# Up projection of a seven-product MLP with joined 512-column matmuls, sums kept in PSUM, and weight sums built in one buffer

## The chip, the core and the metric

The kernel runs on one core of a Trainium2 chip. The metric is the device time of one execution in microseconds (us). Before the change three runs gave 2035.43, 2039.5 and 2040.1 us, a median of 2039.5 us. Five engines work side by side, each on its own list of instructions in order: PE (TensorE, matmuls; its weight loads are listed as PEld), DVE (VectorE), ACT (ScalarE), POOL (GpSimd) and SP (SyncE); the last two issue transfers here. Engines wait for each other through semaphores.

## What is computed

One encoder layer on 512 tokens with 2048 channels in float32: a norm, an input projection, a convolution group and a neighbourhood attention group, an output projection, and then the part that the change touches, a gated MLP with a width-3 convolution over the tokens:

```python
xn = rms_norm(x, ffn_norm_g[l])
up = jnp.einsum("bsd,df->bsf", xn, w_up[l])
up = depthwise_conv(up, ffn_dw_w[l], ffn_dw_b[l])
gate, val = jnp.split(up, 2, axis=-1)
x = x + jnp.einsum("bsf,fd->bsd", jax.nn.silu(gate) * val, w_down[l])
```

The hidden width is 5632, so `w_up` has 2 x 5632 columns.

## The kernel before

**Precision.** Every float32 operand is split into a rounded part (hi) and the rest (lo), and a product is made of three matmuls: hi by hi, hi by lo, lo by hi. `parts` (L112) makes the two weight tiles: ACT writes `whi` (L115) and DVE writes `wlo` (L116), each 128 x 1024. Four buffers exist of each (`NW`).

**Seven products.** The up projection is done as a two-by-two block product with seven multiplications in place of eight. For each of 44 hidden blocks `f` the gate and value columns and the upper and lower channels make the four weight blocks A11, A12, A21, A22; the activations are combined beforehand into seven operands `comb[c]`, each 8 tiles of 128 x 512 (256 columns hi, 256 columns lo). Product `c`, called P0 to P6 here, uses these weights: P3 A11, P0 A22, P5 A12, P1 A22+A21, P2 A21+A11, P4 A22+A21+A11, P6 that and A12. `mm3` (L123) runs a product as 8 x 3 matmuls of 256 columns.

**Order.** `TURN` (L51) is the order of the products inside a block: 3, 0, 1, 4, 5, 2, 6. `plan` is the flat list of weight units; `weights()` (L147) hands out the next one and sees that units are made three ahead (`AHEAD`). So a new `whi` for the product three places on reuses the buffer of the product one place back. Sums of two weight blocks are made by transfer eight units ahead (`FAR`): SP loads one block (L110), POOL adds the second (L588). The sums of three and four blocks are made in place by DVE (L595).

**Results.** P3 stays in PSUM and P4 and P2 are added onto it there; P1 stays in a second bank and P6 is added there; ACT copies four partial results of 256 columns to SBUF (`kept`, L641) and DVE makes the gate half `g` and the value half `vl` from them (L648 to L650). `hidden` (L667) then scales, convolves (L658 to L660), applies SiLU (L672) and multiplies (L673).

**Who decides the order.** Each engine's list is fixed when the program is built: a scheduler takes the instructions by priority and inserts the waits. `sum_ahead` (L170) lets POOL make weight sums for the later down projection, one job at each call: a copy (L176) and an added transfer (L177).

Of the kernel before, what the change touches and what calls it, by code (L numbers as in the profile page):

```python
# [10 lines left out]
F32 = mybir.dt.float32  # L11
F32R = mybir.dt.float32r
AF = mybir.ActivationFunctionType
ALU = mybir.AluOpType
AX = mybir.AxisListType

P = 128
# [30 lines left out]
NW = 4  # L48
NEG = -1.0e30

TURN = (3, 0, 1, 4, 5, 2, 6)  # L51
TURN2 = (3, 0, 4, 1, 2, 6, 5)
Q = D // 2 // S
TAIL = 4
# [16 lines left out]
def layer(ctx: ExitStack, tc: tile.TileContext, xT, w_in, w_out, w_up, w_down, par, tab, g3, out):  # L71
# [17 lines left out]
    def t2(name, dt=F32):  # L89
        return tp.tile([P, S], dt, tag="t2k", name=name)  # L90
# [17 lines left out]
    def raw_unit(src, n):  # L108
        raw = t4([P, U * P], "raw")
        return raw, nc.sync.dma_start(raw[:, :n], src)  # L110
# [8 lines left out]
    def unit(src, n):  # L119

        return parts(raw_unit(src, n)[0], n)[:2]

    def mm3(ps, w, wk, mh, ml, start, stop, more=False):  # L123
        hi, lo = w[:2]
        a = slice(wk * P, (wk + 1) * P)
        nc.tensor.matmul(ps, hi[:, a], mh, start=start, stop=False, skip_group_check=more)  # L126
        nc.tensor.matmul(ps, hi[:, a], ml, start=False, stop=False, skip_group_check=more)  # L127
        return nc.tensor.matmul(ps, lo[:, a], mh, start=False, stop=stop, skip_group_check=more)  # L128
# [18 lines left out]
    def weights():  # L147
        at = weights.at
        weights.at += 1
        for i in range(at, min(at + 1 + FAR, len(plan))):  # L150
            if i in sums:
                sums.pop(i)()
        while len(made) < min(at + 1 + AHEAD, len(plan)):
            made.append(plan[len(made)]())
        return made[at]
# [4 lines left out]

    A11, A12, A21, A22 = range(4)
    wsum = {c: [dram.tile([P, U * P], F32, name=f"ws{c}_{k}") for k in range(NK)] for c in (1, 2, 4, 6)}
    jobs = [(c, k) for k in range(NK) for c in (1, 4, 2, 6)]

    def behind(i, ins):
        tc.add_manual_dep(i.ins, ins.ins.name,
                          mybir.DependencyInfo(mybir.DependencyClass.Sync, mybir.DependencyReason.DATA),
                          reason="behind")

    def sum_ahead(ins):  # L170

        if not jobs:
            return
        c, k = jobs.pop(0)
        a, b = {1: (w_down[k, A22], A21), 2: (w_down[k, A21], A11), 4: (wsum[1][k], A11), 6: (wsum[4][k], A12)}[c]
        behind(nc.gpsimd.dma_start(wsum[c][k], a), ins)  # L176
        nc.gpsimd.dma_start(wsum[c][k], w_down[k, b], accum_op=ALU.add, max_dma_last_dim=ROW)  # L177

    def split(src, g, name):

# [5 lines left out]
    def sum_sq(acc, src, first, to=slice(0, S)):  # L186
        if first:
            nc.scalar.activation(acc, src, AF.Square)
        else:
            q = t2("sq")[:, to]  # L190
            nc.scalar.activation(q, src, AF.Square)
            nc.vector.tensor_add(acc, acc, q)

    def rsqrt_steps(acc, n, name, to=slice(0, S), keep=True):

        m = (to.stop - to.start) // P
        ps = psa.tile([P, 2, S], F32, tag="sc", name="st")[:, 0]
        for i in range(m):
            nc.tensor.matmul(ps[:, i:i + 1], acc[:, to.start + i * P:to.start + (i + 1) * P], ones[:, 0:1],
                             start=True, stop=True)  # L200
        v, r, y = (sm.tile([P, S // P], F32, tag="rs" + c, name="rs" + c)[:, :m] for c in "vry")
        nc.vector.tensor_scalar(v, ps[:, :m], 1.0 / n, EPS, op0=ALU.mult, op1=ALU.add)
        nc.scalar.activation(r, v, AF.Sqrt)
        nc.vector.reciprocal(r, r)
        nc.vector.tensor_mul(y, v, r)
        nc.vector.tensor_mul(y, y, r)
        nc.vector.tensor_scalar(y, y, -0.5, 1.5, op0=ALU.mult, op1=ALU.add)
        nc.vector.tensor_mul(y, y, r)

        dg = t2("dg")  # L210
        for i in range(m):
            nc.vector.tensor_scalar(dg[:, i * P:(i + 1) * P], ident, y[:, i:i + 1], None, op0=ALU.mult)
        yield
        ps = psa.tile([P, 2, S], F32, tag="sc", name="st")[:, 0]
        nc.tensor.matmul(ps[:, :m * P], ones, dg[:, :m * P], start=True, stop=True)
        if not keep:
            return ps[:, :m * P]
        res = t2(name)
        nc.scalar.activation(res[:, to], ps[:, :m * P], AF.Copy)
        return res  # L220
# [273 lines left out]
    def out_half(m, read):  # L494
        for d in range(KD):
            w = weights()
            ps = psm.tile([P, S], F32, tag="mm", name="po2")
            for k in range(U):
                i = mm3(ps, w, k, m[k][0], m[k][1], k == 0, k == U - 1)
            tick(i)  # L500
            if d % 3 == 0:
                sum_ahead(i)
            read(d, ps)
# [73 lines left out]
    def stats2():  # L577
        rstd2.append((yield from rsqrt_steps(acc2, D, "rstd2")))

    def factors(f, at):  # L580

        def load(q):
            a[q] = raw_unit(w_up[f, q], U * P)[0]
            return a[q]

        def summed(c, q1, q2):
            a[c] = raw_unit(w_up[f, q1], U * P)[0]
            nc.gpsimd.dma_start(a[c], w_up[f, q2], accum_op=ALU.add)  # L588

        def make(c):  # L590
            if c in plain:
                return load(plain[c])
            if c in (1, 2):
                return a["s%d" % c]
            add(a["s1"], a["s1"], a[A11 if c == 4 else A12])  # L595
            return a["s1"]

        a = {}
        plain = {0: A22, 3: A11, 5: A12}
        for c, qs in ((1, (A22, A21)), (2, (A21, A11))):  # L600
            sums[at + TURN.index(c)] = lambda c=c, qs=qs: summed("s%d" % c, *qs)
        return [lambda c=c: parts(make(c), U * P)[:2] for c in TURN]

    add = nc.vector.tensor_add
    for f in range(NF):
        plan.extend(factors(f, len(plan)))
    order2 = [*range(NK - KEEP // 2, NK), *range(NK - KEEP // 2)]
    for c in TURN2:
        for k in order2:
            plan.append(lambda c=c, k=k: (unit(wsum[c][k] if c in wsum else w_down[k, {0: A22, 3: A11, 5: A12}[c]],  # L610
                                               U * P), operand(c, k)))

    out_half(mb, after)
    steps.append(stats2())

    def up(f, done):

        def product(c, onto=None):

            w = weights()  # L620
            ps = onto
            if ps is None:
                ps = (psa.tile([P, S], F32, tag="po", name="pu") if c == 1 else
                      psm.tile([P, S], F32, tag="mm", name="pu"))[:, :H]
            for k in range(U):
                m = comb[c][k]
                i = mm3(ps, w, k, m[:, :H], m[:, H:], k == 0 and onto is None, k == U - 1, onto is not None)
            tick(i)
            done(TURN.index(c), i)
            return ps  # L630

        def pair(name):
            return t2(name).rearrange("p (i t) -> p i t", i=2)

        def both(x):
            return x.unsqueeze(1).broadcast_to([P, 2, H])

        vv, uu, v, g = pair("vv"), pair("uu"), pair("vl"), pair("g")

        def kept(t, ps):  # L640
            nc.scalar.activation(t, ps, AF.Copy)  # L641
            return ps

        a = kept(uu[:, 0], product(3))
        kept(vv[:, 0], product(0))
        b = kept(vv[:, 1], product(1))
        kept(uu[:, 1], product(4, a))
        add(g[:, 0], uu[:, 0], product(5))  # L648
        add(v, vv, both(product(2, a)))
        add(g[:, 1], uu[:, 1], product(6, b))  # L650
        g, v = (t.rearrange("p i t -> p (i t)") for t in (g, v))
        return g, v

    def conv3(a, n):
# [24 lines left out]
    def operand(c, k):  # L679

        (b11, b12), (b21, b22) = ((hs[i][:, :H], hs[i][:, H:]) for i in (2 * k, 2 * k + 1))
        if c in (3, 5, 6):
            src = {3: b11, 5: b21, 6: b22}[c]
        else:
            t = t2("hc")
            src, m = t[:, :H], t[:, H:]
            if c == 2:
                nc.vector.tensor_sub(src, b22, b12)
            elif c == 1:
                nc.vector.tensor_sub(src, b11, b12)  # L690
            else:
                nc.vector.tensor_sub(m, b11, b12)
                nc.vector.scalar_tensor_tensor(src, b22, -1.0, m, op0=ALU.mult, op1=ALU.subtract)
                if c == 0:
                    nc.vector.scalar_tensor_tensor(src, src, -1.0, b21, op0=ALU.mult, op1=ALU.subtract)
        t = t2("ho", F32R)
        nc.scalar.activation(t[:, :H], src, AF.Copy)  # L697
        nc.vector.tensor_sub(t[:, H:], src, t[:, :H].bitcast(F32))  # L698
        return t
# [13 lines left out]

    for f in range(NF):
        hidden(f, again if f == NF - 1 else paced)
    assert not jobs and not back

# [193 lines left out]
```

## Time and profile before

| | |
|---|---|
| median of three runs | 2039.5 us |
| profiled execution, its own time | 2037.69 us |
| its span, first to last instruction | 2035.9 us |
| PE busy | 2005.8 us (99%) |
| PEld busy | 1795.3 us (88%) |
| DVE busy | 1593.5 us (78%) |
| ACT busy | 1017.6 us (50%) |
| POOL busy | 227.7 us (11%) |

The span has three stages: projections and attention (to about 708 us), the up projection (to about 1599 us) and the down projection. Matmuls are pipelined, so the busy time of one is longer than the time from its start to the start of the next; the latter is read from the timeline.

### The profile page before, as it was taken

Reading aid. Unit: us, or ns where it says so; the run is one execution under the profiler, and the core shown is the slowest. Engines: PE = TensorE matmul, PEld = TensorE weight load, DVE = VectorE, ACT = ScalarE, POOL = GpSimd, SP = SyncE. Lnnn points to the kernel's source line nnn. Section 1 sums busy time; section 2 is a strip of 40 time slices with the busy share of each in tenths; the row PEclk is TensorE's granted clock in tenths of the full one; section 3 lists DMA queues with packets and bytes.
Section 4 is the critical chain, followed back from the end, with each engine's and each line's share of the span. In section 5 each row is a group of like instructions: output and inputs, shape, how many; then the busy total and the mean of one; then the engine's idle time right before and its main releaser. Section 6 shows DMA issues by size and latency. Waiting matters only on the chain.

```text
span 2035.9 us, 32324 instructions
## 1 busy us (share of the span) xinstructions
PE 2005.8 (99%) x12620; PEld 1795.3 (88%) x12620; DVE 1593.5 (78%) x2223; ACT 1017.6 (50%) x1548; POOL 227.7 (11%) x314
## 2 busy tenths in 40 slices
PE   8999999999999999999999999999999999999997
PEld 6888888877787899999999999999999888888886
DVE  7985798497547878888888888888888698885764
ACT  6234423447525654545455555555455544554663
POOL 0111111011001111111111111111110300000000
PEclk9999999999999999999999999999999999999999
DMA  6676677677757889999999999999886976666563
GB/s 234 167 224 182 171 177 202 181 185 207 227 145 202 206 215 257 239 255 244 252 245 247 258 247 248 245 255 245 237 222 181 341 233 217 213 213 195 191 213 124
DMA packets 140873, 444.96 MB, mean 219 GB/s; under 512 B 15793, under 2 KB 23985, under 8 KB 139313
## 3 DMA queue, kind: packets, MB, share of 16 engines
q1 hardware_dynamic: 97776, 292.94, 42.5%
q0 software_dynamic: 42944, 149.97, 35.3%
q8 instruction: 99, 1.62, 0.3%
q14 instruction: 54, 0.43, 0.1%
HBM read 425.02 MB, written 110.10 MB: 263 GB/s over the span
## 4 chain that ended last, share of the span: by engine, by line
PE 76%; issue 21%; ACT 1%; DMA 1%; DVE 1%; POOL 0%; SPq 0%; POOLq 0%; DVEq 0%
PE pu L126 15%; PE pu L127 15%; PE pu L128 15%; PE pj L126 7%; PE pj L128 6%; PE pj L127 6%; PE po L126 3%; PE po L127 3%; PE po L128 3%; PE po L437 1%; PE sc L397 1%; PE trp L424 1%; DMA raw<-in_w_in 1%; DMA tab<-in_tab 0%; PE trx L537 0%
## 5 line engine op out<-in xcount | busy, mean ns | idle before, releaser
L115 ACT ACTIVATE whi<-raw 128x1024 fp32r<-128x1024 f32 x574 | 606.2, 1057 | 810.7 <-PE pj L127 219.3
L116 DVE TENSOR_TENSOR wlo<-raw,whi 128x1024 fp32r<-128x1024 f32 x574 | 700.7, 1222 | 265.2 <-ACT whi L115 230.4
L126 PE MATMUL pu<-xc,whi 128*128 128x256 f32 x2464 | 697.5, 283 | 1.3 <-ACT uu L641 1.3
L128 PE MATMUL pu<-xc,wlo 128*128 128x256 f32 x2464 | 697.9, 283 | 0.0
L127 PE MATMUL pu<-xc,whi 128*128 128x256 f32 x2464 | 697.7, 283 | 0.0
L126 PEld LDWEIGHTS pu<-xc,whi 128*128 128x128 f32 x2464 | 473.1, 192 | 2.0 <-ACT uu L641 1.7
L128 PEld LDWEIGHTS pu<-xc,wlo 128*128 128x128 f32 x2464 | 473.1, 192 | 0.2 <-issue 0.2
L127 PEld LDWEIGHTS pu<-xc,whi 128*128 128x128 f32 x2464 | 473.2, 192 | 0.1
L126 PE MATMUL pj<-xh,whi 128*128 128x512 f32 x640 | 254.0, 398 | 7.7 <-ACT whi L115 7.7
L128 PE MATMUL pj<-xh,wlo 128*128 128x512 f32 x640 | 251.0, 392 | 1.1 <-DVE wlo L116 1.1
L127 PE MATMUL pj<-xl,whi 128*128 128x512 f32 x640 | 251.3, 393 | 0.0
L737 PE MATMUL pd<-whi,ho 128*128 128x512 f32 x616 | 240.5, 391 | 2.2 <-DVE ho L698 2.2
L735 PE MATMUL pd<-whi,ho 128*128 128x512 f32 x616 | 240.5, 391 | 1.3 <-ACT ho L697 1.3
L736 PE MATMUL pd<-wlo,ho 128*128 128x512 f32 x616 | 240.6, 391 | 0.0
L311 DVE SCALAR_TENSOR_TENSOR y<-ch,prm,y 128x507 f32<-128x507 f32 (+14 forms) x240 | 169.7, 738 | 3.3
L126 PEld LDWEIGHTS pj<-xh,whi 128*128 128x128 f32 x640 | 120.8, 189 | 35.8 <-ACT whi L115 9.0
L128 PEld LDWEIGHTS pj<-xh,wlo 128*128 128x128 f32 x640 | 120.8, 189 | 28.6 <-DVE wlo L116 2.5
L127 PEld LDWEIGHTS pj<-xl,whi 128*128 128x128 f32 x640 | 120.9, 189 | 24.7 <-issue 0.7
L737 PEld LDWEIGHTS pd<-whi,ho 128*128 128x128 f32 x616 | 116.1, 188 | 27.1 <-DVE ho L698 3.0
L735 PEld LDWEIGHTS pd<-whi,ho 128*128 128x128 f32 x616 | 115.9, 188 | 25.7 <-ACT ho L697 1.5
L736 PEld LDWEIGHTS pd<-wlo,ho 128*128 128x128 f32 x616 | 116.0, 188 | 24.9 <-DVE wlo L116 0.6
L177 POOL DMA_DIRECT2D ws<-in_w_down x88 | 79.5, 904 | 360.5 <-DMA ws<-ws 185.1
(161 smaller groups left out, 2029.1 us busy)
## 6 DMA issues: line engine op xcount, KB each, us to landing
raw<-in_w_up SPq DMA_DIRECT2D x220, 512.0 KB, 5.8
ws<-in_w_down POOLq DMA_DIRECT2D x132, 512.0 KB, 7.3
raw<-in_w_up POOLq DMA_DIRECT2D x88, 512.0 KB, 7.9
raw<-ws SPq DMA_DIRECT2D x88, 512.0 KB, 4.2
raw<-in_w_in SPq DMA_DIRECT2D x80, 512.0 KB, 4.8
raw<-in_w_down SPq DMA_DIRECT2D x66, 512.0 KB, 4.0
ws<-ws POOLq DMA_DIRECT2D x44, 512.0 KB, 4.7
raw<-in_w_out SPq DMA_DIRECT2D x32, 512.0 KB, 4.7
```

What stands on the lines that cost most here:

```text
L115: i = nc.scalar.activation(hi[:, :n], raw[:, :n], AF.Copy)
L116: j = nc.vector.tensor_sub(lo[:, :n], raw[:, :n], hi[:, :n].bitcast(F32))
L126: nc.tensor.matmul(ps, hi[:, a], mh, start=start, stop=False, skip_group_check=more)
L127: nc.tensor.matmul(ps, hi[:, a], ml, start=False, stop=False, skip_group_check=more)
L128: return nc.tensor.matmul(ps, lo[:, a], mh, start=False, stop=stop, skip_group_check=more)
L177: nc.gpsimd.dma_start(wsum[c][k], w_down[k, b], accum_op=ALU.add, max_dma_last_dim=ROW)
L311: nc.vector.scalar_tensor_tensor(y[:, a:b], h[:, a + j - PAD:b + j - PAD], prm[:, o + j:o + j + 1], y[:, a:b], op0=ALU.mult, op1=ALU.add)
L397: m = nc.tensor.matmul(both[:, j, i, :], q[hp, b * P:(b + 1) * P], grid(k, KC0[b], KW)[hp], start=True, stop=True)
L424: m = nc.tensor.transpose(ps[:, 2 * i + ch, :], s[:, i, ch * P:(ch + 1) * P], ident)
L735: nc.tensor.matmul(ps[i], h[:, t], wh[:, d], start=start and not more, stop=False, skip_group_check=more)
L736: nc.tensor.matmul(ps[i], h[:, t], wl[:, d], start=False, stop=False, skip_group_check=more)
L737: return nc.tensor.matmul(ps[i], h[:, tl], wh[:, d], start=False, stop=stop, skip_group_check=more)
```

## The change

The order of the products in a block becomes 3, 2, 4, 5, 1, 0, 6. In six of the seven products the first two matmuls of a step (hi weights by the hi half and hi weights by the lo half) become one of 512 columns, whose two halves land in the two halves of a PSUM bank; the third stays at 256 columns. P2 keeps three matmuls of 256. The sums over products are made in five fixed PSUM places that live through the whole stage: `pa` and `pe`, the two halves of one two-bank tile `ea`, and `pd_`, `pb`, `pc_`. P3 runs into `pa`; ACT copies `pa` to `pd_`; P4 runs onto `pa`; ACT copies `pa` to `pe`; P5 runs onto `pd_`; P1 runs onto `pa`; ACT copies `pa` to `pb`; P0 runs onto `pe`; P6 runs onto `pb`. `folded` adds the two halves of a bank into SBUF (ACT copies the right half, DVE adds the left). Three matmuls ahead of the stage write the places that are later added to. The weight sums start from A21+A11 (P2's): A22 is added for P4, A12 for P6; A22 is kept for P0.

Beside this, the jobs of `sum_ahead` are taken product by product, with the added transfer of a job issued after the copy of the next, and the statistics of the second norm use another PSUM tag (`stat`).

```diff
-TURN = (3, 0, 1, 4, 5, 2, 6)
+TURN = (3, 2, 4, 5, 1, 0, 6)
...
-    jobs = [(c, k) for k in range(NK) for c in (1, 4, 2, 6)]
+    jobs = [(c, k) for c in (1, 4, 2, 6) for k in range(NK)]
+    open_job = []
...
     def sum_ahead(ins):
 
-        if not jobs:
-            return
-        c, k = jobs.pop(0)
-        a, b = {1: (w_down[k, A22], A21), 2: (w_down[k, A21], A11), 4: (wsum[1][k], A11), 6: (wsum[4][k], A12)}[c]
-        behind(nc.gpsimd.dma_start(wsum[c][k], a), ins)
-        nc.gpsimd.dma_start(wsum[c][k], w_down[k, b], accum_op=ALU.add, max_dma_last_dim=ROW)
+        job = jobs.pop(0) if jobs else None
+        if job:
+            c, k = job
+            a = {1: w_down[k, A22], 2: w_down[k, A21], 4: wsum[1][k], 6: wsum[4][k]}[c]
+            behind(nc.gpsimd.dma_start(wsum[c][k], a), ins)
+        if open_job:
+            c, k = open_job.pop()
+            nc.gpsimd.dma_start(wsum[c][k], w_down[k, {1: A21, 2: A11, 4: A11, 6: A12}[c]], accum_op=ALU.add,
+                                max_dma_last_dim=ROW)
+        if job:
+            open_job.append(job)
...
-            if c in (1, 2):
-                return a["s%d" % c]
-            add(a["s1"], a["s1"], a[A11 if c == 4 else A12])
-            return a["s1"]
+            if c == 1:
+                return a[1]
+            if c == 4:
+                add(a[2], a[2], load(A22))
+            elif c == 6:
+                add(a[2], a[2], a["q", A12])
+            return a[2]
...
+    ea = psa.tile([P, 2, S], F32, tag="sc", name="pu")
+    pd_, pb, pc_ = (psm.tile([P, S], F32, tag="mm", name="pu") for _ in range(3))
+    pe, pa = ea[:, 0], ea[:, 1]
+    for x in (pe, pd_, pb):
+        nc.tensor.matmul(x, comb[3][0][:, :P], comb[3][0], start=True, stop=True)
...
+        def product(c, ps, more):
+            hi, lo = wt = weights()
             for k in range(U):
-                m = comb[c][k]
-                i = mm3(ps, w, k, m[:, :H], m[:, H:], k == 0 and onto is None, k == U - 1, onto is not None)
+                m, w = comb[c][k], slice(k * P, (k + 1) * P)
+                if c == 2:
+                    i = mm3(ps[:, :H], wt, k, m[:, :H], m[:, H:], k == 0, k == U - 1)
+                    continue
+                nc.tensor.matmul(ps, hi[:, w], m, start=k == 0 and not more, stop=False, skip_group_check=more)
+                i = nc.tensor.matmul(ps[:, :H], lo[:, w], m[:, :H], start=False, stop=k == U - 1,
+                                     skip_group_check=more)
...
+        def copied(to, ps):
+            with shifted(-100):
+                nc.scalar.activation(to, ps, AF.Copy)
+
+        def folded(to, ps):
+            nc.scalar.activation(to, ps[..., H:], AF.Copy)
+            add(to, to, ps[..., :H])
+
+        product(3, pa, False)
+        copied(pd_, pa)
+        product(2, pc_, False)
+        w = t2("w")[:, :H]
+        nc.scalar.activation(w, pc_[:, :H], AF.Copy)
+        product(4, pa, True)
+        copied(pe, pa)
+        product(5, pd_, True)
+        g = t2("g")
+        folded(g[:, :H], pd_)
+        product(1, pa, True)
+        copied(pb, pa)
+        product(0, pe, True)
+        v = t2("vl")
+        by = v.rearrange("p (i t) -> p i t", i=2)
+        folded(by, ea)
+        add(by, by, w.unsqueeze(1).broadcast_to([P, 2, H]))
+        product(6, pb, True)
+        folded(g[:, H:], pb)
```

Line numbers of the changed kernel that the prediction uses: L652 and L653 are the 512-column and the 256-column matmul of `product`, L660 is `copied`, L663 and L664 are the copy and the add of `folded`, L682 the add of `w`; L115 and L116 keep their numbers.

More of the change, by code (lines that the diff above doesn't have):

```diff
@@ L192, in sum_sq, with stat @@
             nc.vector.tensor_add(acc, acc, q)
+    def stat():
+        if where:
+            return psa.tile([P, S], F32, tag="tr", name="st", bufs=2)
+        return psa.tile([P, 2, S], F32, tag="sc", name="st")[:, 0]
+    where = []
     def rsqrt_steps(acc, n, name, to=slice(0, S), keep=True):
         m = (to.stop - to.start) // P
-        ps = psa.tile([P, 2, S], F32, tag="sc", name="st")[:, 0]
+        ps = stat()
         for i in range(m):
@@ L213, in rsqrt_steps @@
         yield
-        ps = psa.tile([P, 2, S], F32, tag="sc", name="st")[:, 0]
+        ps = stat()
         nc.tensor.matmul(ps[:, :m * P], ones, dg[:, :m * P], start=True, stop=True)
@@ L582, in load @@
         def load(q):
-            a[q] = raw_unit(w_up[f, q], U * P)[0]
-            return a[q]
+            a["q", q] = raw_unit(w_up[f, q], U * P)[0]
+            return a["q", q]
         def summed(c, q1, q2):
@@ L590, in make @@
         def make(c):
+            if c in plain and ("q", plain[c]) not in a:
+                load(plain[c])
             if c in plain:
-                return load(plain[c])
-            if c in (1, 2):
-                return a["s%d" % c]
-            add(a["s1"], a["s1"], a[A11 if c == 4 else A12])
-            return a["s1"]
+                return a["q", plain[c]]
+            if c == 1:
[5 more added lines that the diff above has]
+            return a[2]
         a = {}
         plain = {0: A22, 3: A11, 5: A12}
-        for c, qs in ((1, (A22, A21)), (2, (A21, A11))):
-            sums[at + TURN.index(c)] = lambda c=c, qs=qs: summed("s%d" % c, *qs)
+        sums[at + TURN.index(2)] = lambda: summed(2, A21, A11)
+        sums[at + TURN.index(1)] = lambda: summed(1, A22, A21)
         return [lambda c=c: parts(make(c), U * P)[:2] for c in TURN]
@@ L607, in layer, with unit2 @@
     order2 = [*range(NK - KEEP // 2, NK), *range(NK - KEEP // 2)]
+    def unit2(c, k):
+        return unit(wsum[c][k] if c in wsum else w_down[k, {0: A22, 3: A11, 5: A12}[c]], U * P)
     for c in TURN2:
         for k in order2:
-            plan.append(lambda c=c, k=k: (unit(wsum[c][k] if c in wsum else w_down[k, {0: A22, 3: A11, 5: A12}[c]],
-                                               U * P), operand(c, k)))
+            plan.append(lambda c=c, k=k: (unit2(c, k), operand(c, k)))
     out_half(mb, after)
+    where.append(1)
@@ L614, in layer @@
     steps.append(stats2())
-    def up(f, done):
[L618 to L624, printed above, removed]
-            for k in range(U):
-                m = comb[c][k]
-                i = mm3(ps, w, k, m[:, :H], m[:, H:], k == 0 and onto is None, k == U - 1, onto is not None)
+    ea = psa.tile([P, 2, S], F32, tag="sc", name="pu")
@@ L628, in product @@
             tick(i)
             done(TURN.index(c), i)
[L630 to L651, printed above, removed]
+        def copied(to, ps):
[5 more added lines that the diff above has]
+        product(3, pa, False)
@@ L715, in layer @@
         hidden(f, again if f == NF - 1 else paced)
-    assert not jobs and not back
+    assert not jobs and not open_job and not back
     def four(first):
```

## The prediction

> **What bounds the kernel now.** I read the page first (shares, chain, groups), then a window over the middle of the up projection, then the timeline of each engine inside it.
>
> ```profile
> span 2035.9 us, 32324 instructions
> ...
> PE 2005.8 (99%) x12620; PEld 1795.3 (88%) x12620; DVE 1593.5 (78%) x2223; ACT 1017.6 (50%) x1548; POOL 227.7 (11%) x314
> ...
> PE 76%; issue 21%; ACT 1%; DMA 1%; DVE 1%; POOL 0%; SPq 0%; POOLq 0%; DVEq 0%
> ```
>
> ```profile
> 740.00:1580.00 840.00, 840.00 (x7002) 840.00 (x7002) 697.74 (x792) 435.69 (x583) 127.36 (x158) 1.00 0.92 242
> ```
>
> The columns of the window are length, then PE, PEld, DVE, ACT and POOL busy with counts, granted clock, transfer share, GB/s. PE is busy for the whole 840 us at clock 1.00, and 7002 matmuls in it make one per 119.97 ns. DVE (83%), ACT (52%) and the transfers (0.92) keep up. So PE's issue of matmuls sets the time of the stage, and what counts is how many matmuls there are and whether PE ever waits.
>
> ```profile
> 1002.57 0.33 SPq L675 DMA_DIRECT2D h<-uy  x1
> ...
> 1022.72 0.33 SPq L675 DMA_DIRECT2D h<-uy  x1
> ```
>
> Two stores of a finished block lie 20.15 us apart: 168 matmuls of 119.97 ns (20.155 us), with nothing between.
>
> **Fewer matmuls: the gain.** The down projection runs the same kind of matmul at 512 columns:
>
> ```profile
> 1700.15 0.39 PE L735 MATMUL pd<-whi,ho 128*128 128x512 f32 x1
> ...
> 1703.55 0.39 PE L735 MATMUL pd<-whi,ho 128*128 128x512 f32 x1
> ```
>
> Between these starts lie 15 steps: 226.7 ns each. The 256 additional columns cost 106.7 ns, so each matmul carries 13.3 ns besides its columns. A changed block has 48 of 512 columns, 48 of 256 and P2's 24 of 256: 48 x 226.7 + 72 x 119.97 = 19.52 us against 20.155. That is 0.637 us a block, 28.0 us over 44 blocks. No row shows a 512 and a 256 in turn; the pair's bounds are 320 ns (columns alone, 56 us more gained) and 360 ns (three of 256, nothing gained). I take the sum of the two cadences, which fits both.
>
> [...]
>
> **A new wait: P1 to P0.** The compiled order of the changed kernel, the same in all 44 blocks, has on ACT (left) and PE (right) at the end of P1:
>
> ```
> ACT L115 whi for the next P2    waits: transfer, P1's last L652    PE  8 x (L652, L653) of P1, onto pa
> ACT L660 pb <- pa               waits: P1's last L653              PE  2 x 256 of the next P2 (wait: that whi)
> ACT L115, L663 vl <- ea         wait: P0                           PE  L652 of P0, onto pe, waits: L660 pb <- pa
> ```
>
> P0 writes `pe`, the copy reads `pa`; but both are halves of the tile `ea`, and the program orders them. P0 stands directly behind P1, so nothing but two small matmuls covers the copy, and the copy stands on ACT behind a 1024-column `whi` that cannot start until P1's last hi matmul frees its buffer. The other copies (P3 to P4, P4 to P1) have a whole product between. The profile before has this very pattern once, at the stage's start:
>
> ```profile
> 720.99 0.28 PE L127 MATMUL pu<-xc,whi 128*128 128x256 f32 x1
> 721.11 0.28 PE L128 MATMUL pu<-xc,wlo 128*128 128x256 f32 x1
> ...
> 722.69 0.39 PE L126 MATMUL pu<-xc,whi 128*128 128x256 f32 x1 [1.30 <-ACT uu L641]
> 722.92 0.28 PE L127 MATMUL pu<-xc,whi 128*128 128x256 f32 x1
> ```
>
> ```profile
> 721.31 1.06 ACT L115 ACTIVATE whi<-raw 128x1024 fp32r<-128x1024 f32 x1 [1.11 <-PE pu L127]
> 722.28 0.36 ACT L641 ACTIVATE uu<-pu 128x256 f32<-128x256 f32 x1
> ```
>
> From it: the copy starts 0.97 us after `whi`; PE starts 0.05 us after the copy ends (722.28 + 0.36); the first matmul takes 0.23 us to the next start in place of 0.12, 0.11 more. How long after a last 512-column hi matmul `whi` starts:
>
> ```profile
> 494.46 0.39 PE L127 MATMUL pj<-xl,whi 128*128 128x512 f32 x1
> ```
>
> ```profile
> 494.89 1.06 ACT L115 ACTIVATE whi<-raw 128x1024 fp32r<-128x1024 f32 x1 [2.48 <-PE pj L127]
> ```
>
> 0.43 us after its start. A copy from PSUM to PSUM has no row; the nearest of 512 columns reads PSUM, the bounds are one of 256 columns and the slowest of 512:
>
> ```profile
> L428 ACT ACTIVATE pt<-trp 128x512 f32<-128x512 f32 x32 | 17.3, 590 | 10.0 <-PE trp L424 10.0
> L641 ACT ACTIVATE vv<-pu 128x256 f32<-128x256 f32 x88 | 32.6, 373 | 55.1 <-PE pu L128 55.1
> L658 ACT ACTIVATE uy<-g,prm 128x512 f32<-128x512 f32 x44 | 35.9, 815 | 0.0
> ```
>
> I take 0.59. Counted from the start of P1's last hi matmul, P0 starts at 0.43 + 0.97 + 0.59 + 0.05 = 2.04. Without a wait it would start at 0.227 + 0.120 + 2 x 0.120 = 0.587 (the two P2 matmuls are not lost: `whi` ends at 1.49 and they run under the copy). Lost: 2.04 - 0.587 + 0.11 = 1.56 us a block, 68.6 us in 44 blocks (1.34 to 1.79 by the bounds of the copy, 59 to 79 us). PE is queued here itself; ACT's and DVE's work behind shifts with it.
>
> **A second wait, P6 to the next P3.** P3 overwrites `pa`, so it waits for DVE's L664 add that reads `ea`. Ahead of that add on DVE stand the sum L611 and a `wlo`, whose `whi` waits for P0's last hi matmul.
>
> ```profile
> 1017.09 1.22 DVE L116 TENSOR_TENSOR wlo<-raw,whi 128x1024 fp32r<-128x1024 f32 x1
> 1018.23 0.74 DVE L659 SCALAR_TENSOR_TENSOR uy<-g,prm,uy 128x511 f32<-128x511 f32 x1
> ```
>
> ```profile
> L649 DVE TENSOR_TENSOR vl<-vv,pu 128x512 f32<-128x512 f32 x44 | 30.2, 687 | 28.9 <-PE pu L128 28.9
> L673 DVE TENSOR_TENSOR uy<-uy 128x512 f32<-128x512 f32 x44 | 30.1, 684 | 0.0
> ```
>
> From P0's start: last hi matmul at 0.11 + 7 x 0.347 = 2.54, `whi` 2.97 to 4.03, `wlo` from 4.08, the add 1.14 later (5.22) for 0.69, P3 free at 5.96. PE gets there at 0.11 + 2 x 2.773 + 2 x 0.12 = 5.90. The slack is gone: 0.06 to 0.17 us, I take 0.1, 43 times: 4.3 us.
>
> **What lies beside PE.** Per block DVE gains one 512-column add (L682, as L673: 0.68 us); ACT gains three copies to PSUM, 512 + 2 x 256 columns of folding and one of 256 for `w`, and loses four of 256: 2.0 us. On the longer block (19.52 + 1.56 + 0.1 = 21.2 us) that is 16.7 + 0.7 = 17.4 on DVE (82%) and 10.5 + 2.0 = 12.5 on ACT (59%): covered. The two other copies, walked the same way: P3's copy to `pd_` ends 2.54 + 0.43 + 0.97 + 0.59 = 4.53 us after P3's start, and PE comes to P4 after P3 (2.88) and 20 matmuls of P2 (2.40) at 5.28: 0.7 us to spare. P4's copy to `pe` stands on ACT behind the SiLU of the block before, which waits for DVE's convolution. From P0's start DVE's list runs from the add at 5.22 through two sums, four scalings and adds, two `wlo` and three convolution steps to 13.5; SiLU (0.6), `whi` (0.97) and the copy (0.59) end at 15.7, and PE comes to P1 at 16.8: 1 us to spare. Neither waits.
>
> ```profile
> raw<-in_w_up SPq DMA_DIRECT2D x220, 512.0 KB, 5.8
> ...
> raw<-in_w_up POOLq DMA_DIRECT2D x88, 512.0 KB, 7.9
> ```
>
> Transfers keep their number. By the same walk SP's loads of A22 and A12 are issued some 11 us before DVE wants them, against 5.8 to land, and POOL's added sums some 29 us ahead, against 5.8 + 0.9 + 7.9. The jobs of `sum_ahead` are wanted in the down projection alone, and each added transfer still stands behind its own copy on POOL, so that part, `stat` and the new order of `halves` I cost at nothing; without the cover a late sum costs PE one landing, some 8 us. The three matmuls ahead of the stage: 3 x 0.227 = 0.7 us. The stage's end has one more copy of 256 on ACT ahead of the first operand: 1 us (0 to 2). The wait at 722 quoted above goes, since the sum has 44 new ones: -1.5 us.
>
> **The sum.** 2037.7 (the profiled execution's own time; 1.8 around its span) - 28.0 + 68.6 + 4.3 + 0.7 + 1.0 - 1.5 = 2082.8. That execution lies 1.8 us under the median of the runs, so against the runs 2085.
>
> **The rivals.**
>
> 1. Not slower: P0 isn't held at P1's end. The order that the program asks for is real, but the semaphore would have to be reached early, as by the copy to `pe`, which ends over 2 us before. For it: 840 us without any PE wait, though copies of partial sums are made there too. Against: the wait's value is the later copy's. The gain stays, 2085 - 68.6 - 4.3 = 2012. It decides below a wait of 0.54 us a block ((28.0 - 4.3)/44).
> 2. Only the copy counts, `whi` being out of its way: 0.51 + 0.04 + 0.59 + 0.05 - 0.587 + 0.11 = 0.71 us a block, 2085 - 37 = 2048.
> 3. The clock. Windows with long PE idle are followed by half clock:
>
> ```profile
> 500.00:503.40 3.40, 1.40 (x9) 1.06 (x10) 3.21 (x6) 1.89 (x7) 0.91 (x1) 0.99 0.89 361
> 503.30:506.80 3.50, 3.50 (x12) 2.64 (x11) 1.62 (x4) 2.98 (x7) 0.00 (x0) 0.51 1.07 348
> ...
> 1599.00:1602.40 3.40, 1.51 (x8) 0.87 (x7) 1.84 (x4) 1.98 (x4) 0.89 (x2) 1.00 1.01 394
> 1602.40:1605.80 3.40, 3.40 (x9) 2.61 (x9) 2.85 (x7) 0.00 (x0) 1.56 (x3) 0.50 1.02 398
> ```
>
> ```profile
> 720.00:725.00 5.00, 3.70 (x26) 3.01 (x25) 4.49 (x12) 2.08 (x5) 0.99 (x1) 1.00 0.60 193
> ```
>
> PE busy for 1.40 and 1.51 of 3.4 us was followed by 0.5 for 3.4 us; 1.3 us idle at 721 was not. The new wait leaves about 1.1 us idle in that measure, between them, nearer the harmless case. If it tripped whenever a wait falls inside one such window (1.9/3.4 of 44 = 25 times 1.7 us): 2085 + 42 = 2127. [...]
> 4. DVE's add comes later than walked, by one more 256-column add's 0.3 us: 43 x 0.3 = 13, 2098.
> 5. The change doesn't do what it says: a 512 and a 256 take as long as three of 256. 2085 + 28 = 2113.
>
> **How the numbers follow.** Forecast 0.68, rivals in turn 0.08, 0.04, 0.10, 0.07, 0.03. The forecast's own range is 2072 to 2098 (copy 59 to 79 us, end, second wait). The 8 in 10 range takes in rivals 4 and 5: 2067 to 2113; rivals 1, 2 and most of 3 lie outside. Counting 0.3% (6 us) as what a measurement tells from no change: faster 0.08, same 0.02 (the low edge of rival 2), slower 0.90.
>
> **What would show it.** A store of a block every 21.2 us in place of 20.15. Starts of L652 and L653 alternating at 227 and 120 ns (rival 5 otherwise). In PE's waits a group of 44 for ACT L660 with some 1 us of modelled idle each, the chain there running through ACT L115 and L660; absent, rival 1, and the forecast falls by 70 us. L660 at about 0.59 us. P3 released by DVE L664 with under 0.2 us. Granted clock 1.00 in the stage's middle (rival 3 otherwise).

## The result, and the profile after

The changed kernel takes 2089.8 us, median of 4 runs (2089.56 to 2091.84), against 2039.5 us (2035.43 to 2040.1): ratio 1.025, 95% interval [1.024, 1.027]. The forecast was 2085 us in 2067 to 2113. The profiled execution took 2091.84 us.

The page of the changed kernel: span, then PE, PEld, DVE, ACT and POOL busy, then the chain that ended last, by engine and by line.

```profile
span 2090.1 us, 28359 instructions
...
PE 2015.7 (96%) x10511; PEld 1687.4 (81%) x10511; DVE 1602.6 (77%) x2267; ACT 1090.8 (52%) x1680; POOL 228.5 (11%) x314
...
PE 74%; issue 20%; ACT 3%; DMA 1%; DVE 1%; POOL 0%; SPq 0%; POOLq 0%; DVEq 0%; ACTq 0%
PE pu L652 24%; PE pu L653 12%; PE pj L126 6%; PE pj L128 6%; PE pj L127 6%; PE po L126 3%; PE po L127 3%; PE po L128 3%; ACT whi L115 3%; PE pu L126 3%; PE pu L128 2%; PE pu L127 2%; PE po L450 1%; PE sc L410 1%; PE trp L437 1%
```

There are 2109 matmuls fewer, as the change says (48 x 44 = 2112, three added), yet PE is 10 us longer busy and 44 us more of the span lie between its matmuls. ACT's share of the chain went from 1 to 3%, and `whi` is a line of the chain. PE's waits (total, times, longest) and the middle of the stage say where:

```profile
PE pu L126 <- ACT whi L115: 44.3, 43, 1.0
...
PE pu L652 <- ACT pu L660: 1.5, 1, 1.5
```

```profile
740.00:1640.00 900.00, 856.77 (x5036) 742.19 (x5036) 709.15 (x840) 509.75 (x714) 130.25 (x163) 1.00 0.83 226
```

44 waits, one a block, in a stretch in which PE never idled before; the clock stays at 1.00. All but one of these waits name `whi`; the copy is waited for too, by PE's weight loads (PEld):

```profile
L652 PEld LDWEIGHTS pu<-xc,whi 128*128 128x128 f32 x2112 | 396.7, 188 | 103.8 <-ACT pu L660 9.9
```

The 9.9 us are 44 waits, 1.8 us in the last block and 0.19 in each other, behind the wait for `whi`. The queue of stores gives the period of a block:

```profile
1021.95 0.33 SPq L708 DMA_DIRECT2D h<-uy  x1
1043.41 0.33 SPq L708 DMA_DIRECT2D h<-uy  x1
```

21.46 us against 20.15: 1.31 us a block, 57.6 us in 44 blocks. The place is the end of P1. PE's timeline there (start, length, line; in brackets the idle time ahead and its releaser), with two rows that bound an undisturbed stretch of P0 and the first step of the next P3, behind P6:

```profile
1025.49 0.40 PE L652 MATMUL pu<-xc,whi 128*128 128x512 f32 x1
...
1027.03 0.39 PE L126 MATMUL pu<-xc,whi 128*128 128x256 f32 x1 [1.03 <-ACT whi L115]
1027.26 0.28 PE L127 MATMUL pu<-xc,whi 128*128 128x256 f32 x1
1027.52 0.50 PE L652 MATMUL pu<-xc,whi 128*128 128x512 f32 x1
1027.85 0.28 PE L653 MATMUL pu<-xc,wlo 128*128 128x256 f32 x1
...
1028.32 0.40 PE L652 MATMUL pu<-xc,whi 128*128 128x512 f32 x1
...
1030.44 0.40 PE L652 MATMUL pu<-xc,whi 128*128 128x512 f32 x1
...
1033.51 0.48 PE L652 MATMUL pu<-xc,whi 128*128 128x512 f32 x1
1033.83 0.28 PE L653 MATMUL pu<-xc,wlo 128*128 128x256 f32 x1
```

and ACT's timeline beside it:

```profile
1025.92 1.06 ACT L115 ACTIVATE whi<-raw 128x1024 fp32r<-128x1024 f32 x1 [1.50 <-PE pu L652]
1026.89 0.58 ACT L660 ACTIVATE pu<-pu 128x512 f32<-128x512 f32 x1
```

`whi` starts 0.43 us after P1's last hi matmul, the copy 0.97 later, and P0 starts 0.05 after the copy's end (1027.52): 2.03 us behind that hi matmul. Without a wait it would be there after a pair (0.353) and two matmuls of P2 (0.24); with the longer first step (0.33 in place of 0.23) the block loses 2.03 - 0.59 + 0.10, about 1.53 us. PE's bracket names `whi`, not the copy: the two matmuls of the next P2, which the compiled order has ahead of P0, take the idle stretch on themselves, and the rest lies between 1027.26 and 1027.52 without a bracket.

Between 1028.32 and 1030.44 lie six pairs of a 512 and a 256: 353.3 ns a pair. P3's first step is 0.32 us in place of 0.23, the second wait. The block adds up: 48 x 0.3533 + 24 x 0.12 + 1.53 + 0.09 = 21.46 us.

### The profile page after: what moved, and what is told of

Same layout as the page of the kernel before. It is cut to its first block, busy times and chain, and to the rows that moved or that the text cites. A ratio compares the mean times of both kernels' runs of the same rounds, so it can differ in the third digit from the quotient of the medians.

```text
span 2090.1 us, 28359 instructions
## 1 busy us (share of the span) xinstructions
PE 2015.7 (96%) x10511; PEld 1687.4 (81%) x10511; DVE 1602.6 (77%) x2267; ACT 1090.8 (52%) x1680; POOL 228.5 (11%) x314
## 4 chain that ended last, share of the span: by engine, by line
PE 74%; issue 20%; ACT 3%; DMA 1%; DVE 1%; POOL 0%; SPq 0%; POOLq 0%; DVEq 0%; ACTq 0%
PE pu L652 24%; PE pu L653 12%; PE pj L126 6%; PE pj L128 6%; PE pj L127 6%; PE po L126 3%; PE po L127 3%; PE po L128 3%; ACT whi L115 3%; PE pu L126 3%; PE pu L128 2%; PE pu L127 2%; PE po L450 1%; PE sc L410 1%; PE trp L437 1%
## 5 line engine op out<-in xcount | busy, mean ns | idle before, releaser
L115 ACT ACTIVATE whi<-raw 128x1024 fp32r<-128x1024 f32 x574 | 606.9, 1058 | 867.7 <-PE pu L652 310.7
L116 DVE TENSOR_TENSOR wlo<-raw,whi 128x1024 fp32r<-128x1024 f32 x574 | 697.2, 1221 | 377.3 <-ACT whi L115 354.5
L652 PE MATMUL pu<-xc,whi 128*128 128x512 f32 x2112 | 760.5, 403 | 1.5 <-ACT pu L660 1.5
L653 PE MATMUL pu<-xc,wlo 128*128 128x256 f32 x2112 | 593.1, 281 | 0.0
L652 PEld LDWEIGHTS pu<-xc,whi 128*128 128x128 f32 x2112 | 396.7, 188 | 103.8 <-ACT pu L660 9.9
L653 PEld LDWEIGHTS pu<-xc,wlo 128*128 128x128 f32 x2112 | 399.0, 189 | 0.3 <-issue 0.2
L126 PE MATMUL pu<-xc,whi 128*128 128x256 f32 x352 | 104.2, 296 | 44.8 <-ACT whi L115 44.3
L601 POOL DMA_DIRECT2D raw<-in_w_up x88 | 89.5, 1017 | 507.6 <-DMA raw<-in_w_up 233.2
```

Of the source, the lines that this page charges most:

```text
L115: i = nc.scalar.activation(hi[:, :n], raw[:, :n], AF.Copy)
L116: j = nc.vector.tensor_sub(lo[:, :n], raw[:, :n], hi[:, :n].bitcast(F32))
L652: nc.tensor.matmul(ps, hi[:, w], m, start=k == 0 and not more, stop=False, skip_group_check=more)
L653: i = nc.tensor.matmul(ps[:, :H], lo[:, w], m[:, :H], start=False, stop=k == U - 1, skip_group_check=more)
```

## The experiments

Each run is the changed kernel with the edit shown; the last three start from the version with two tiles, as they say. The kernel before, run beside them, took medians of 2036.8 to 2037.8 us.

**A tile each for pe and pa.**

```diff
-    ea = psa.tile([P, 2, S], F32, tag="sc", name="pu")
+    pa = psa.tile([P, 2, S], F32, tag="sc", name="pu")[:, 0]
+    pe = psa.tile([P, S], F32, tag="po", name="pu")
...
-    pe, pa = ea[:, 0], ea[:, 1]
...
-        folded(by, ea)
+        folded(by[:, 0], pe)
+        folded(by[:, 1], pa)
```

> The accumulators pe and pa get a tile each (one bank each) in place of the halves of one tile, and the two folds are done apart, so that nothing orders P0's first matmul behind the copy pb<-pa. Theory (the wait of P0 is an order between two banks that share a tile, 1.53 us in each of 44 blocks): 2089.8 - 44 x 1.53 = 2022 us, block period 21.46 - 1.53 = 19.9 us, and the row of PE waiting 43 times for ACT whi before P0 is gone; faster than the kernel before by 0.8%. Rival (the copy and whi are only what ended last, and PE would wait as long for its weights or for DVE): 2080 to 2095 us, with another wait of about 1.5 us between P1 and P0. Rival (the denser PE loses its clock): granted clock below 0.97 in the up stage and 2060 us or more. What the smaller folds cost more on ACT (two of 0.37 for one of 0.58 us) and DVE lies beside PE by all three.

Measured: 2019.8 us (2018.52 to 2021.18), ratio to the kernel before 0.991 [0.990, 0.993]. PE at P1's last hi matmul, P0's first and two later ones, and ACT beside them, in the timelines of this run:

```profile
1022.97 0.40 PE L652 MATMUL pu<-xc,whi 128*128 128x512 f32 x1
...
1023.32 0.40 PE L652 MATMUL pu<-xc,whi 128*128 128x512 f32 x1
...
1024.38 0.40 PE L652 MATMUL pu<-xc,whi 128*128 128x512 f32 x1
...
1024.73 0.40 PE L652 MATMUL pu<-xc,whi 128*128 128x512 f32 x1
```

```profile
1024.37 0.58 ACT L660 ACTIVATE pu<-pu 128x512 f32<-128x512 f32 x1
1024.88 0.37 ACT L663 ACTIVATE vl<-pu 128x256 f32<-128x256 f32 x1
```

P0 starts 0.35 us behind P1's last hi matmul, one pair, and PE goes on at 0.35 us a pair while ACT copies `pa` and even begins to fold it: P0 does not need either. The two matmuls of the next P2 no longer stand ahead of P0. The queue of stores shows the period:

```profile
1019.20 0.46 SPq L709 DMA_DIRECT2D h<-uy  x1
1039.03 0.33 SPq L709 DMA_DIRECT2D h<-uy  x1
```

19.83 us, 1.63 less than 21.46: the first wait (1.53) and the second, P3 behind the joint add (0.09). 44 x 1.63 = 71.7 us; the medians differ by 70.1. So the whole wait was an order between two PSUM banks that were one tile to the program: in this run PE adds onto `pe` while ACT reads `pa`, and 70 us of order were not needed.

**Weights two ahead in place of three**, in the up stage alone.

```diff
-        while len(made) < min(at + 1 + AHEAD, len(plan)):
+        while len(made) < min(at + 1 + weights.ahead, len(plan)):
...
+    weights.ahead = 2
```

> The weights of the up stage are made two products ahead instead of three, so that whi of the next block's P2, which waits for P1's last matmul, is no longer in front of the copy pb<-pa on ACT; pe and pa stay halves of one tile. Theory (the wait has two parts, whi 0.8 to 0.9 us and the copy 0.6 to 0.7 us): 2089.8 - 44 x 0.84 = 2053 us, with P0 waiting 0.7 us for ACT L660 in each block. Rival (only the copy counts, and whi would have been out of its way): no change, 2085 to 2095 us. Rival (two ahead is too late and PE waits for its weights somewhere else): over 2095 us, with a new row of PE waiting for ACT whi at other products.

Measured: 2093.5 us (2090.82 to 2094.24), ratio 1.027 [1.026, 1.029]. A miss that says nothing on the rivals, since ACT's order did not change:

```profile
1026.09 1.06 ACT L115 ACTIVATE whi<-raw 128x1024 fp32r<-128x1024 f32 x1 [1.50 <-PE pu L655]
1027.05 0.58 ACT L663 ACTIVATE pu<-pu 128x512 f32<-128x512 f32 x1
```

`whi` can start when P1's last hi matmul ends, the copy one lo matmul later. That the compiled order takes what is ready first, whichever product it was made for, would explain it but is not shown. The order itself had to be set:

**whi behind the copy.** The weights made at P0 are issued behind the copy `pb<-pa`.

```diff
-        copied(pb, pa)
-        product(0, pe, True)
+        product(0, pe, True, copied(pb, pa))
...
+                with tc.issue_after(behind.ins):
+                    hi, lo = wt = weights()
```

> pe and pa stay halves of one tile, and the one whi that was in front of the copy pb<-pa on ACT is put behind it; with that the two matmuls of the next block's P2 between P1 and P0 fall back into their own place. The run with weights two ahead left this order as it was, so it said nothing on it. Theory (the 1.53 us have two parts, and the copy alone is 0.58 us and the way to it and back): P0 loses 0.7 us a block, 2089.8 - 44 x 0.8 = 2054 us, and PE waits for the copy (ACT L664) before P0. Rival (only the copy counts; whi lay in its shadow): 2085 to 2095 us. Rival (the whi moved back comes too late for the next block, or the idle stretch moves the clock): over 2095 us.

Measured: 2064.2 us (2063.49 to 2065.22), ratio 1.013 [1.012, 1.015]. PE and ACT at P1's end:

```profile
1015.71 0.40 PE L656 MATMUL pu<-xc,whi 128*128 128x512 f32 x1
...
1016.96 0.50 PE L656 MATMUL pu<-xc,whi 128*128 128x512 f32 x1 [0.73 <-ACT pu L664]
```

```profile
1016.32 0.58 ACT L664 ACTIVATE pu<-pu 128x512 f32<-128x512 f32 x1 [1.67 <-PE pu L657]
1016.82 1.05 ACT L115 ACTIVATE whi<-raw 128x1024 fp32r<-128x1024 f32 x1
```

The wait has two parts. `whi` ahead of the copy is worth 2089.8 - 2064.2 = 25.6 us, 0.58 a block, the second wait's 0.09 in it. What is left is 2064.2 - 2019.8 = 44.4 us, 1.01 a block: P0 starts 1.25 us behind P1's last hi matmul in place of 0.353 (0.90), and its first step is 0.10 longer. The run was expected at 2054 us: P2's two matmuls (0.24 us) no longer run inside the pause, which was not in that sum. The second wait went along, although the tile is still shared. DVE's timeline shows why:

```profile
1020.71 0.69 DVE L668 TENSOR_TENSOR vl<-vl,pu 128x512 f32<-128x512 f32 x1 [0.33 <-ACT vl L667]
...
1022.04 1.22 DVE L116 TENSOR_TENSOR wlo<-raw,whi 128x1024 fp32r<-128x1024 f32 x1
```

The add that frees `pa` (L668 here) now stands ahead of the `wlo`, 1.2 us earlier in the order, and P3 follows P6 without a longer step (22 pairs in a row at 353 ns from P0 on).

**The copy twice.**

```diff
         copied(pb, pa)
+        copied(pb, pa)
```

> The copy pb<-pa behind P1 is issued twice. Theory (this copy is on the path that sets the end, once a block): 44 x 0.58 = 25.5 us more, 2115 us. Rival (P0 waits for something else, the copy ends in its shadow): under 5 us more, below 2095 us. If the wait were for whi alone, the second copy would cost nothing too.

Measured: 2163.7 us in one run. PE's timeline has P1's last hi matmul, P0's first two, and one further on:

```profile
1049.20 0.40 PE L652 MATMUL pu<-xc,whi 128*128 128x512 f32 x1
...
1051.84 0.50 PE L652 MATMUL pu<-xc,whi 128*128 128x512 f32 x1 [0.60 <-ACT pu L660]
...
1052.30 0.40 PE L652 MATMUL pu<-xc,whi 128*128 128x512 f32 x1
...
1057.15 0.39 PE L652 MATMUL pu<-xc,whi 128*128 128x512 f32 x1
```

The copy is on the path: P0 starts 2.64 us behind P1's last hi matmul in place of 2.03, and 44 x 0.61 = 27 us. But 74 us came, and the granted clock of the stage fell to 0.95, which neither expectation of this run had (the prediction's third rival had it for the change itself). The six stretches at half clock from 867 to 1011 us in this trace last 3.41 us each and start 7, 13, 7, 7 and 7 times 3.41 us apart, as on a grid. Windows cut on that grid, around two pauses of the same length:

```profile
863.97:867.38 3.41, 1.78 (x9) 1.20 (x8) 2.12 (x3) 2.12 (x3) 0.00 (x0) 1.00 1.01 231
867.38:870.79 3.41, 3.41 (x12) 2.83 (x12) 0.39 (x1) 0.00 (x0) 0.00 (x0) 0.50 0.91 336
...
908.34:911.75 3.41, 3.03 (x18) 2.37 (x16) 1.59 (x3) 1.79 (x3) 1.16 (x2) 1.00 0.99 309
911.75:915.17 3.42, 2.18 (x11) 1.80 (x12) 2.45 (x2) 1.66 (x3) 0.00 (x0) 1.00 1.10 268
915.17:918.58 3.41, 3.41 (x21) 3.00 (x21) 1.02 (x1) 1.54 (x2) 0.00 (x0) 1.00 0.63 251
```

The first pause falls whole into one window of the grid (PE busy 1.78 of 3.41 us), and the clock is halved in the next. The second is cut in two (3.03 and 2.18), and the clock stays. So it goes in eight pauses of this trace, at 866 and from 912 to 1051 us: the five behind a window with 1.78 to 1.80 us busy are followed by half clock, and the three whose windows have 1.91 us or more are not. In the whole stage of this trace 31 of the 44 pauses are followed by half clock. From pause to pause in PE's rows a block with a halved stretch takes 23.59 us (from 958.02) and one without 22.03 (from 1028.71), so 31 x 1.56 = 48 us; with the 27 it makes the 74, but for 1 us.

**Half of the copy twice**, a dose between the two.

```diff
         copied(pb, pa)
+        copied(pb[:, :H], pa[:, :H])
```

> The changed kernel, with the first 256 columns of the copy pb<-pa copied a second time, so that P0 starts some 0.3 us later in each block (the whole copy twice made it 0.6 us, and the clock fell to 0.95 in the stage). Theory (the path alone, clock stays): 2089.8 + 44 x 0.3 = 2103 us at a granted clock of 1.00. Rival (a longer pause of any size lowers the clock in proportion): about 2126 us at 0.97. Rival (the fall is a step that lies between 2.0 and 2.3 us of pause): 2135 us or more at 0.95 to 0.97.

Measured: 2109.2 us in one run, clock 1.00 in the stage. PE's timeline:

```profile
1031.54 0.40 PE L652 MATMUL pu<-xc,whi 128*128 128x512 f32 x1
...
1033.97 0.50 PE L652 MATMUL pu<-xc,whi 128*128 128x512 f32 x1 [0.38 <-ACT pu L660]
```

P0 starts 2.43 us behind P1's last hi matmul, 0.40 more than in the changed kernel: 2089.8 + 44 x 0.40 = 2107 us. A window with the pause in it, and the one behind:

```profile
1075.00:1078.40 3.40, 1.99 (x11) 1.33 (x10) 2.10 (x4) 1.91 (x3) 0.93 (x2) 1.00 1.06 315
1078.40:1081.80 3.40, 3.40 (x21) 2.98 (x20) 0.87 (x2) 1.15 (x2) 0.00 (x0) 1.00 1.15 359
```

With 1.99 of 3.4 us busy the clock stays at 1.00 here. So, in these two single runs, a pause of 2.43 us in this measure left the clock of the stage at 1.00 and one of 2.64 us came with 0.95, which is no price in proportion. The changed kernel's pause, 2.03, is 0.40 us shorter than the one that left it.

**The old order of the weight sums' jobs.**

```diff
-    jobs = [(c, k) for c in (1, 4, 2, 6) for k in range(NK)]
-    open_job = []
+    jobs = [(c, k) for k in range(NK) for c in (1, 4, 2, 6)]
```

with the body of `sum_ahead` as before the change.

> The changed kernel with the weight sums of the down stage issued in the order of before (one product of all four per k, the accumulating transfer right behind its first one). Theory (this part of the change lies beside PE and is worth nothing): 2089.8 us within 0.3% (2083 to 2096). Rival (its transfers meet the loads of the up weights, and the new order hides part of the loss): over 2096 us. Rival (the new order is itself a loss): below 2083 us.

Measured: 2090.0 us (2088.59 to 2090.88), ratio 1.026 [1.024, 1.027]. This part is worth nothing, as costed.

**The joined matmuls taken apart**, in the version with two tiles and for the five products that add onto something.

```diff
-                nc.tensor.matmul(ps, hi[:, w], m, start=k == 0 and not more, stop=False, skip_group_check=more)
+                for h in (slice(0, H), slice(H, S)) if more else (slice(0, S),):
+                    nc.tensor.matmul(ps[:, h], hi[:, w], m[:, h], start=k == 0 and not more, stop=False,
+                                     skip_group_check=more)
```

> The version with a tile each for pe and pa, and in five of the six joined products (all but P3, 40 pairs a block) each matmul of 512 columns with the high weights is two of 256 columns again. Theory (the pair 512+256 takes 353.4 ns as its rows show, three of 256 take 359.9 ns): 2019.8 + 40 x 44 x 6.5 ns = 2031 us. Rival (the forecast's pair of 346.7 ns holds, and what makes it 353.4 ns weighs on three of 256 too): 2019.8 + 40 x 44 x 13.3 ns = 2043 us. Rival (joining saves nothing): 2020 us.

Measured: 2031.3 us (2028.86 to 2033.66, 10 runs), ratio 0.997 [0.996, 0.998]. Starts of the hi matmuls in PE's timeline (x2: two of 256 columns in one row):

```profile
1020.32 0.40 PE L653 MATMUL pu<-xc,whi 128*128 128x256 f32 x2
...
1020.68 0.40 PE L653 MATMUL pu<-xc,whi 128*128 128x256 f32 x2
```

360 ns for three of 256, as before the change. 2031.3 - 2019.8 = 11.5 us for 40 pairs a block, 6.5 ns a pair; P3's 8 pairs stay joined here, and scaled to all 48 it makes an estimated 13.8 us. That is what joining is worth, not 28.

**Less change of width.** In the version with two tiles, first all eight hi matmuls of a product and then its eight lo ones; and, in a second run, two hi and then two lo.

```diff
-                i = nc.tensor.matmul(ps[:, :H], lo[:, w], m[:, :H], start=False, stop=k == U - 1,
-                                     skip_group_check=more)
+            for k, w in enumerate(cols if c != 2 else ()):
+                i = nc.tensor.matmul(ps[:, :H], lo[:, w], comb[c][k][:, :H], start=False, stop=k == U - 1,
+                                     skip_group_check=more)
```

> The version with a tile each for pe and pa, and in each of the six joined products first all eight matmuls of 512 columns with the high weights, then all eight of 256 with the low ones, in place of one after the other. Theory (a change of width between neighbours costs 6.6 ns a pair; rows of one width run at 226.7 and 119.97 ns): 2019.8 - 48 x 44 x 6.6 ns = 2006 us, with neighbours of 512 columns 226.7 ns apart. Rival (the 6.6 ns are the price of a matmul of 512 in this stage, whatever stands beside it): 2020 us, with neighbours of 512 at 233.4 ns. Rival (wlo, needed later, and whi, free earlier, move ACT and DVE so that a wait arises): over 2024 us.

> As the run with all eight high matmuls first, but two of 512 columns and then two of 256, so half as many changes of width as in the split version. Theory (a price for each change of width): half the gain, 2019.8 - 7 = 2013 us. Rival (a price of the 512 matmul itself): 2020 us. Rival (the cadence falls on steps, and four matmuls together reach the fast one whole): 2006 us.

Measured: 2011.3 us (2009.09 to 2013.61), ratio 0.987 [0.986, 0.989], for eight and eight; 2010.5 us (2010.3 to 2011.69), ratio 0.987 [0.986, 0.989], for two and two. PE's timeline, eight and eight:

```profile
1021.79 2.00 PE L653 MATMUL pu<-xc,whi 128*128 128x512 f32 x8
1023.63 1.11 PE L655 MATMUL pu<-xc,wlo 128*128 128x256 f32 x8
1024.58 2.00 PE L653 MATMUL pu<-xc,whi 128*128 128x512 f32 x8
```

and two and two:

```profile
1019.99 0.63 PE L653 MATMUL pu<-xc,whi 128*128 128x512 f32 x2
...
1028.35 0.63 PE L653 MATMUL pu<-xc,whi 128*128 128x512 f32 x2
```

2.79 us for eight pairs is 348.8 ns a pair; 8.36 us for 24 pairs is 348.3 ns. Two and two, with half the changes of width, reaches the whole of what eight and eight has (48 x 44 x 5.0 ns = 10.6 us by the rows, 9.3 by the medians). So the 6.6 ns by which 353.3 exceeds the two pure cadences (346.7) are neither a price for each change of width (that would have halved) nor the 512 matmul's own (that would have stayed). Both versions beat the kernel before by 1.3%.

## Why the prediction was right, and what it had wrong

**Fewer matmuls: the gain of 28.0 us** was the mis-sized term. The step "I take the sum of the two cadences" had 346.7 ns for a 512 and a 256 in turn; the rows have 353.3, inside the bounds of 320 and 360. The gain is 48 x 44 x 6.5 ns, 13.8 us, scaled from the matmuls taken apart. Rival 5 (360 ns) was nearly as far off on its side.

**A new wait: P1 to P0, 68.6 us** was right in place, cause and size. Its steps against the rows: whi 0.43 behind the hi matmul (0.43), copy 0.97 later (0.97), copy 0.59 (0.58), PE 0.05 later (0.05), P0 at 2.04 (2.03); 1.56 us a block became 1.53. That the shared tile is the cause was read from the compiled order and is shown by the two tiles. That both `whi` and the copy count, is shown by the order turned round, 25.6 us for the one (the second wait's 4 in it) and 44.4 for the other. One sign came out otherwise: the group of 44 waits for L660 stands with PE's weight loads and is 0.19 us in most, not some 1 us; the 1 us rows, and the chain of the page, name `whi`.

**A second wait, P6 to the next P3, 4.3 us**: P3's first step is 0.32 us in place of 0.23, 0.09 a block, 3.9 us. DVE's add in the changed kernel:

```profile
1032.76 0.68 DVE L664 TENSOR_TENSOR vl<-vl,pu 128x512 f32<-128x512 f32 x1
```

It begins 5.24 us behind P0's start (5.22 forecast) and P3 starts at 5.99 (5.96). The cause is the one given: where the order turned round puts the add ahead of the `wlo`, the wait is gone.

**What lies beside PE** was right: the only other wait with a row in the stage is one of 0.6 us at its start, DVE is 79% busy in the stage's middle and ACT 57% (82 and 59 forecast), and the old order of jobs gave 2090.0 us.

**The stage's end, +1.0**, was wrong in sign. PE waits 1.6 us in place of 1.3 for the first operand there, but another wait of the down projection went. Before, and then after, in PE's waits:

```profile
PE pd L737 <- DVE ho L698: 2.2, 2, 1.6
```

```profile
PE pd L770 <- DVE ho L731: 0.6, 1, 0.6
```

From the last up matmul to the end of the span it is 434.7 us (from 1655.4) against 436.6 (from 1599.3): -1.9, of which these waits explain 1.3.

**The sum** for a profiled execution was 2082.8 and came out at 2091.84: +13.9 for the pair, -1.7 for the two waits, -2.9 for the end make +9.3. The profile of before lay 1.8 us under its median, that of after 2.0 us above, so that the medians miss by 4.8 only. That closeness is in part luck: the pair alone was 14 us off, the other terms took 5 of it back, and the scatter of the two profiled executions nearly 4.

**The rivals.** 1 is out: the hold was real and worth 70 us. 2 did not happen, `whi` stood in the way; run as a kernel it took 2064 and not 2048 us. It had P2's two matmuls inside the pause, and they moved away with `whi` (0.24 us a block, 11 us); the copy began 0.61 us behind the hi matmul in place of 0.55 (3 us); and it had the pair's 14 us too much of gain. The second wait that went and the shorter end give 7 us of it back, so that some 5 us stay open. 3 did not happen (clock 1.00), but what it describes was seen: in single runs, a pause 0.6 us longer brought it, with some 47 us, while 0.4 us did not. And, as that rival has it, not every pause did it: 31 of 44 in that run, and of its eight pauses named above the five that fall whole into one window. 4 did not happen. 5 was half true: half of the gain went.

## What to carry to other kernels

Where accumulators that live side by side are halves of one tile, look in the compiled order for a matmul that waits for a reader of the other half: a tile each was worth 70 us here, more than the 17 us by which the change then beats the kernel before. Walk a copy between engines from the event that frees its engine, with what stands ahead of it in that engine's order, and not by its own length alone: 0.58 us of copy, behind 0.97 us of weights, cost 1.53 us. Take the cadence of a mix of matmuls from rows of that mix; the sum of two pure cadences missed half of a gain of 28 us.

## What the hardware showed that was not expected

A 512- and a 256-column matmul in turn take 353.3 ns, two and two 348.3, eight and eight 348.8, while the pure cadences of before add up to 346.7. For some stretches after a pause the plain alternation too runs at 347 ns (in the run with the copy twice, from 1052.30 to 1057.15, fourteen pairs at 346.4 ns, and from 1030.62 to 1034.78, twelve at 346.7) and then goes back to 353 (from 1041.07 to 1048.84, 22 pairs at 353.2). That looks like two states of one stream; what sets them stays open.

In the run with the copy twice the clock fell behind idle times far shorter than the 3.41 us of a halved stretch: 1.63 us idle within one window of the grid halved it, and the same pause cut in two by the grid left it. Busy time alone does not tell the two cases apart: in the changed kernel's own trace a window of 3.41 us from 497.89 us, on the grid of that trace's half-clock stretches at 504.72 and 1658.43, had 1.68 us busy, and the clock stayed at 1.00 in it and in the next. What the clock counts stays open. In the run with the copy twice it fell with no single idle stretch over 1.03 us around 867, by the profile's brackets.
